# Two more modulation units from TensorE to VectorE beside the first mixer's heads, fed from the weights' buffers

## The chip, the cores and the metric

The kernel runs on one core of a Trainium2 chip. The metric is the device time of one execution in microseconds (us), taken as the median of several runs. The names used below are those of the profile: PE is TensorE, DVE is VectorE, ACT is ScalarE, POOL is GpSimd, and SP is the engine whose queue issues all the large DMAs.

## The reference

One inference step of a two-layer backbone. Both groups of 128 tokens (a prompt and a latent sample) pass through the same weights; the model width is 2048. Cut to what matters here:

```
for l in range(DEPTH):
    mod = jax.nn.silu(cond) @ w_ada[l] + b_ada[l]
    sh1, sc1, gt1, sh2, sc2, gt2 = jnp.split(mod[:, None, :], 6, axis=-1)
    h = rmsnorm(x, g_norm_mix[l]) * (1 + sc1) + sh1
    m, new = mixer_ab(h, ...) if l % 2 == 0 else mixer_c(h, ...)
    x = x + gt1 * m
    h = rmsnorm(x, g_norm_ffn[l]) * (1 + sc2) + sh2
    x = x + gt2 * conv_ffn(h, ...)
```

`mod` is a product of two condition vectors (one for each group) with a matrix of 2048 x 12288 per layer. It has only two rows of output, so its cost is that of bringing 100 MB of `w_ada` per layer through the core. It depends on nothing but the condition, so the kernel spreads it over the stages ahead of its use.

`mixer_ab` makes, from one input projection, queries and keys for eight heads of latent attention (which need two further small products, `w_q_up` and `w_kv_up`) and eight heads of grouped-query attention. An output projection `w_out` of 2048 x 2048 follows.

## The kernel before, in words

**Products.** Every weight tile of 128 x 2048 numbers (1024 KB) is loaded by SP into a buffer called `raw`, of which there are three, and then split in two halves of 1024 columns: ACT writes the rounded high part `wh` (L241), DVE the rest `wl` (L242). There are four buffers each for `wh` and `wl`. `gemm` (L393, L394, L397) then issues three matmuls for each block of 128 x 128. A product of the output projection, which will be called a chunk here, is 16 blocks and so 48 matmuls of 256 columns.

**Modulation units.** A unit is one of the six vectors of a layer, `j`, and a quarter of its 2048 outputs, `q`; it is four tiles of `w_ada`, 1024 KB each. There are three ways to do one.
- On PE (`row_step`, `sum_rows`, L526): a tile is loaded into one of two buffers `araw`; four matmuls with the condition as a narrow stationary matrix sum it into a PSUM tile, four column groups at a time; after four tiles ACT copies the result out, and four transposes (L477) turn it.
- On DVE by the row queue (units whose place in `ROWS` is in `SUMMED`): the tile is loaded in another layout, into the same `araw`, and DVE multiplies it with the condition, which lies in `condb` for each partition, and sums along the row (`feature_sum`, L503). A tile takes two such instructions, one for each condition vector.
- On DVE by the list `FEATS`, in the same way, from buffers of their own.

The rows of `ROWS` have numbers: 8 to 11 are the gate of the first mixer, 12 to 15 the scale of the first FFN, 16 and 17 half of its shift. Of these only unit 10 is in `SUMMED` before the change. The units are pushed on by `pump`, which stands after each product and advances the row queue by a rate (`RATE`, 0.85 in the heads, 0.7 in the output projection of this mixer; four steps to a tile at one step for 0.25).

**The heads** are the loop `for h in range(0, 8, 2)` of `mixer_ab`, from about 195 us of the profile on. Each of its four rounds has three products with `w_q_up`, two with `w_kv_up` and one by token for the values, and starts the attention of four heads. Their outputs go to `o`, a tile of 16 rows by the name `hx`; DVE's feature sums need a place for products that nobody reads, and took `o[:, 4:8]` for it until round h = 4.

**The output projection** follows: 16 chunks with `gemm(W.chunk(), oh, ol, first=8)`, each followed by `residual` (two DVE instructions, L667), by the row units that are left, and by two units of `FEATS` on DVE at 1.3 feature sums to a chunk. The last three chunks (`QUIET`) have none of these, and their splits are made in pieces of 512 columns. Then the sum of squares goes to PE (L221, L222), and the modulation of the FFN's input begins.

A scheduler orders the instructions of each engine ahead of time; where the code says `keep_in_program_order`, as for feature sums, the instruction keeps its place among others that say so. At run time each engine and the SP queue work strictly in that order.

Of the kernel before, what the change touches and what calls it, by code (L numbers as in the profile page):

```python
# [11 lines left out]
F32R = mybir.dt.float32r  # L12
# [6 lines left out]
P = 128  # L19
# [61 lines left out]
FEATS += [(1, 5, 1), (1, 5, 2), (1, 5, 3)]  # L81
RLIMIT = {"ab": 18, "ffn0": 19, "c": 30, "ffn1": 31}
FLIMIT = {"ab": 2, "ffn0": 14, "c": 14, "ffn1": 17}
SUMMED = [10, 20, 21, 22, 24, 25, 26, 29]
INV = {2048: 0, 768: 1, 512: 2, 128: 3, 256: 4}


# [1 line left out]
def step_kernel(ctx: ExitStack, tc: tile.TileContext, A: dict):  # L89
# [22 lines left out]
    def T_(pl, shape, tag, dt=F32, bufs=None):  # L112
        kw = {} if bufs is None else {"bufs": bufs}
        return pl.tile(shape, dt, tag=tag, name=nm(tag), **kw)
# [29 lines left out]
    act.activation(condw[:, :, 0:2], C("cond").rearrange("p (k r) -> p k r", r=2), AF.Silu)  # L144

    condb = T_(keep, [P, 2, D], "condb")

    def load_cw(l):
        ada["cw"] = T_(keep, [P, 4, 2 * NFF], "convw")
# [372 lines left out]
    def sum_rows(t, raw, ps=None):  # L522
        if t == 0:
            ada["ps"] = ps or T_(ppool["ada"], [P, 512], "ada", bufs=1)
        for g in range(4):
            i = pe.matmul(ada["ps"][32 * g:32 * g + 32, :], condw[:, 4 * t + g, :], raw[:, g],  # L526
                          start=(t == 0), stop=(t == 3), skip_group_check=True)
            if pinned[0]:
                tc.keep_in_program_order(i)

    def row_step(until=len(ROWS)):
        if later:
            later.pop(0)()
        if ada["i"] >= until:
            return
        l, j, q = ROWS[ada["i"]]
        t, g = divmod(ada["t"], 4)
        on_dve = ada["i"] in SUMMED
        if g == 0:
            ada["raw"] = T_(wpool, [P, 4, 512], "araw", bufs=2)  # L540
            sp.dma_start(out=ada["raw"], in_=A["w_ada"][l, j, q, t])
        raw = ada["raw"]
        if on_dve:
            if g % 2:
                feature_sum((l, j, q), t, g // 2, raw, ada["junk"]())
        elif pinned[0]:
            if g == 1 and t:
                sum_rows(t - 1, ada["last"])
            if g == 3:
                ada["last"] = raw  # L550
                if t == 3:
                    last = ada["last"]
                    later.append(lambda: None)
                    later.append(lambda: sum_rows(3, last))
        elif g == 3:
            sum_rows(t, raw)
        ada["t"] += 1
        if ada["t"] == 16:
            later.extend([lambda: biased(l, j, q)] if on_dve else ada_finish(l, j, q))
            ada["i"] += 1  # L560
            ada["t"] = 0

    def pump(rows, feats=0.0, until=None):

        until = until or RLIMIT[stage[0]]
        step()
        ada["due"] += rows
        while ada["due"] >= 0.25:
            if ada["i"] >= until and not later:
                ada["due"] = 0.0  # L570
                break
            dve_or_none = ada["i"] >= until or ada["i"] in SUMMED
            ada["due"] -= 0.25 if dve_or_none else 0.25 * ada["pew"]
            row_step(until)
        feat["due"] += feats
        while feat["due"] >= 1.0 and feat["i"] < FLIMIT[stage[0]]:
            feat["due"] -= 1.0
            feature_step()
# [46 lines left out]
    def modulated(st, l, which, W, fixed):  # L625
# [12 lines left out]
            return raw  # L638

        raws = [load_tile(0), load_tile(1)]  # L640
        hx = T_(keep, [P, KD, ROW], "hx", F32R)
        r = stat_rstd(st, D, att_bank)
        sum_rows(0, raws[0], bank())
        rb = spread(diagonal(r, (0, 1)), bank=att_bank)
# [91 lines left out]
    def mixer_ab(hx, W, units, st):  # L736
        l = 0
        with tc.tile_pool(name="ab", bufs=1) as ab:
# [275 lines left out]

            with tc.tile_pool(name="abh", bufs=1, reuse_waits="tile") as hp:
                ada["pew"] = PEW["heads"]
                ada["junk"] = lambda: o[:, 4:8]

                o = T_(keep, [P, KD, ROW], "hx", F32R)
                load_cw(0)  # L1020
                WQ = Weights(A["w_q_up"], 6, 2)
                WK = Weights(A["w_kv_up"], 4, 4)
# [29 lines left out]
                for h in range(0, 8, 2):  # L1052
                    for i in range(2):
                        ps = gemm(WQ.chunk(), qh, qlo)
                        qn[i] = T_(hp, [P, NT], "qn", bufs=3)
                        act.copy(qn[i], ps)
                        if h == 0:
                            for half in (slice(0, D // 2), slice(D // 2, D)):
                                act.activation(condb[:, i, half], condb[:, i, half], AF.Silu)
                        pump(RATE["heads"])  # L1060
# [3 lines left out]
                    qr = T_(hp, [P, NT], "qr", bufs=2)  # L1064
                    act.copy(qr[:, 0:T], ev[:, 0:T])
                    rope(qr[:, None, T:], ev[:, None, T:], 1, 32, "rcm", "rsm")
                    pump(RATE["heads"])
                    kn = []
                    for i in range(2):
                        if h + i < 7:  # L1070
                            start(gqa_query(h + i + 1))
                        start(gqa(h + i))
                        ps = gemm(WK.chunk(), kh, klo, 3 * T)
                        kn.append(T_(hp, [P, 3 * T], "kn", bufs=2))
                        act.copy(kn[i], ps)
                        pump(RATE["heads"])
                    if h == 0:
                        query_scale()
# [6 lines left out]
                        by_token(wide, xs, [out], True, True)  # L1085
                    act.copy(vs[:, :2 * NT], two)
                    act.copy(vs[:, 2 * NT:], one[:, :NT])
                    pump(RATE["heads"])
                    if h == 4:
                        ada["junk"] = None  # L1090
                    start(mla(h, qn[0], qr, kn[0], vm))
                    pump(RATE["heads"])
                    start(mla(h + 1, qn[1], qr, kn[1], vm))
                flush()
# [200 lines left out]
    with banks("pab") as ppool["ada"]:  # L1295
# [3 lines left out]
        for u in units[:2]:  # L1299
            u.load(1, tc.keep_in_program_order)  # L1300
            u.load(0, tc.keep_in_program_order)
            W.fetch(tc.keep_in_program_order)
        hx = T_(keep, [P, KD, ROW], "hx", F32R)
        st = stat_init()
        mixer_ab(hx, W, units, st)
        W = Weights(A["w_up"][0], KD, 1)
# [169 lines left out]
```

## Time and profile before

| what | value |
|---|---|
| runs | 2314.3, 2315.39, 2316.38 us; median 2315.39 |
| profiled execution, its own time | 2317.66 us |
| span in its profile | 2315.9 us |
| mean granted clock of PE | 0.993 |
| DVE busy | 1826.2 us (79%) |
| ACT busy | 1177.5 us (51%) |
| DMA | 610.82 MB, mean 264 GB/s |

The page of the profile says how busy each engine is over the span; the windows say the same for chosen stretches, with the granted clock, the mean busy share of the 16 DMA engines and the rate. A timeline lists instructions by start, with duration; where equal ones follow each other they are one row with a count, and the duration is then that of the whole row. Matmuls overlap, so what one costs is the distance from its start to the start of the next kind, not its duration. In these records a matmul of `L526` or of the attention stands twice: a tile's four matmuls are eight records.

### The profile page before, as it was taken

What the parts mean: (1) busy time and instruction counts of PE and PEld (TensorE: products, weight loads), DVE (VectorE), ACT (ScalarE), POOL (GpSimd) and SP (SyncE); (2) the same over time, 40 slices, a digit from 0 to 9 for tenths busy, and PEclk for the clock granted to TensorE, in tenths of its full rate; (3) what the DMA queues carried; (4) which work ended last, traced back from release to release, by engine and by line L of the source; (5) the groups of instructions that cost most, each with busy time, mean ns of one, the idle gap of its engine ahead of it and who ended that gap; (6) DMA issues with size and microseconds to landing.
All of it is one profiled execution on the core that took longest, in us unless ns stands there. A gap on an engine that the chain in (4) does not pass through costs nothing. (4 is left out here: it accounts for less than half of the span.)

```text
span 2315.9 us, 47404 instructions
## 1 busy us (share of the span) xinstructions
PE 2274.8 (98%) x19812; PEld 2183.7 (94%) x19812; DVE 1826.2 (79%) x2651; ACT 1177.5 (51%) x1869; POOL 145.9 (6%) x132
## 2 busy tenths in 40 slices
PE   8999999999999999999999999999999999999998
PEld 6888878799999999999989999898999999999998
DVE  5667749789989999999879989797899755666654
ACT  4347654555543455554465555446555434555553
POOL 0011101200000000002210000022000000000011
PEclk9999999999999999999999999999999999999999
DMA  9997889667768877777667788885667555555553
GB/s 391 386 370 274 300 310 394 239 250 258 258 253 308 291 259 271 256 260 274 267 244 280 285 316 293 297 307 220 251 247 266 199 186 198 199 186 198 196 188 127
DMA packets 92566, 610.82 MB, mean 264 GB/s; under 512 B 9984, under 2 KB 17856, under 8 KB 20544
## 3 DMA queue, kind: packets, MB, share of 16 engines
q1 hardware_dynamic: 92352, 607.80, 70.8%
q8 instruction: 155, 2.54, 0.4%
q14 instruction: 59, 0.48, 0.1%
HBM read 603.01 MB, written 4.75 MB: 262 GB/s over the span
## 5 line engine op out<-in xcount | busy, mean ns | idle before, releaser
L241 ACT CAST wh<-raw 128x1024 fp32r<-128x1024 f32 (+1 forms) x790 | 792.5, 1010 | 919.8 <-PE acc L394 700.2
L242 DVE TENSOR_TENSOR wl<-raw,wh 128x1024 fp32r<-128x1024 f32 (+1 forms) x790 | 923.7, 1185 | 300.7 <-ACT wh L241 292.5
L393 PE MATMUL acc<-hx,wh 128*128 128x256 f32 x3440 | 952.7, 277 | 1.4 <-ACT wh L241 0.8
L397 PE MATMUL acc<-hx,wl 128*128 128x256 f32 x3440 | 951.4, 277 | 0.2 <-DVE wl L242 0.2
L394 PE MATMUL acc<-hx,wh 128*128 128x256 f32 x3440 | 951.5, 277 | 0.0
L393 PEld LDWEIGHTS acc<-hx,wh 128*128 128x128 f32 x3440 | 646.1, 188 | 8.6 <-issue 5.9
L397 PEld LDWEIGHTS acc<-hx,wl 128*128 128x128 f32 x3440 | 645.5, 188 | 5.5 <-issue 3.4
L394 PEld LDWEIGHTS acc<-hx,wh 128*128 128x128 f32 x3440 | 646.2, 188 | 1.0 <-issue 0.8
L503 DVE CUSTOM_DVE_ANT_0 junk<-araw,condb 128x2048 f32<-128x2048 f32 (+1 forms) x192 | 442.7, 2306 | 0.1
L394 PE MATMUL acc<-g,wh 128*128 128x256 f32 x1408 | 388.3, 276 | 0.0
L397 PE MATMUL acc<-g,wl 128*128 128x256 f32 x1408 | 388.0, 276 | 0.0
L393 PE MATMUL acc<-g,wh 128*128 128x256 f32 x1408 | 387.8, 276 | 0.0
L394 PEld LDWEIGHTS acc<-g,wh 128*128 128x128 f32 x1408 | 264.3, 188 | 0.0
L397 PEld LDWEIGHTS acc<-g,wl 128*128 128x128 f32 x1408 | 264.2, 188 | 0.0
L393 PEld LDWEIGHTS acc<-g,wh 128*128 128x128 f32 x1408 | 264.1, 188 | 0.0
L190 POOL TENSOR_TENSOR sqacc<-sqacc,sq 128x256 f32<-128x256 f32 x61 | 81.8, 1341 | 1573.2 <-issue 1213.4
L914 PE MATMUL acc<-hx,wh 128*128 128x256 f32 x608 | 112.3, 285 | 1.0 <-ACT hx L884 0.6
L914 PEld LDWEIGHTS acc<-hx,wh 128*128 128x128 f32 x608 | 93.0, 189 | 9.4 <-issue 4.9
L1247 ACT ACTIVATE cv<-acc,convw 128x256 f32<-128x256 f32 x176 | 98.2, 558 | 2.5 <-PE acc L381 2.5
L667 DVE SCALAR_TENSOR_TENSOR x<-acc,mod,x 128x128 f32<-128x128 f32 x192 | 57.9, 342 | 40.9 <-PE acc L397 39.9
L1253 DVE SCALAR_TENSOR_TENSOR cv<-acc,convw,cv 128x254 f32<-128x254 f32 x176 | 84.3, 479 | 3.7
L1250 DVE SCALAR_TENSOR_TENSOR cv<-acc,convw,cv 128x254 f32<-128x254 f32 x176 | 83.5, 474 | 2.5 <-ACT cv L1247 2.5
(276 smaller groups left out, 2489.8 us busy)
## 6 DMA issues: line engine op xcount, KB each, us to landing
raw<-w_up SPq DMA_DIRECT2D x176, 1024.0 KB, 4.8
araw<-w_ada SPq DMA_DIRECT2D x160, 1024.0 KB, 5.3
raw<-w_down SPq DMA_DIRECT2D x88, 1024.0 KB, 4.8
raw<-w_in_c SPq DMA_DIRECT2D x48, 1024.0 KB, 5.6
raw<-w_in_ab SPq DMA_DIRECT2D x20, 1024.0 KB, 12.2
araw<-w_first SPq DMA_DIRECT2D x16, 1024.0 KB, 8.2
condb<-w_first SPq DMA_DIRECT2D x16, 1024.0 KB, 9.3
raw<-w_out_ab SPq DMA_DIRECT2D x16, 1024.0 KB, 7.8
```

The costliest lines, as they stand in the source:

```text
L190: pool.tensor_tensor(out=st["acc"], in0=st["acc"], in1=sq, op=ALU.add)
L241: pin(act.copy(out_hi, src))
L242: pin(dve.tensor_tensor(out=out_lo, in0=src, in1=out_hi.bitcast(F32), op=ALU.subtract))
L393: fixed(pe.matmul(ps[:, :n], wh, xh(k), start=(i == 0), stop=False))
L394: fixed(pe.matmul(ps[:, :n], wh, xl(k), start=False, stop=False))
L397: fixed(pe.matmul(ps[:, :n], wl, xh(k), start=False, stop=(i == last)))
L503: tc.keep_in_program_order(dve.tensor_tensor_reduce(out=junk, in0=raw, in1=condb[:, c].rearrange("p (g n) -> p g n", g=4), scale=1.0, scal ...
L667: dve.scalar_tensor_tensor(out=x[:, c, s], in0=ps[:, s], scalar=mod[:, l, 3 * which + 2, c, g:g + 1], in1=x[:, c, s], op0=ALU.mult, op1=AL ...
L914: pin(pe.matmul(ps, w, hx[:, k, lo:lo + NT], start=first and k == ks[0] and n == 0, stop=last and k == ks[-1] and n == 2, skip_group_check ...
L1247: pin(act.activation(y, ps, AF.Identity, scale=cw[:, 1, m:m + 1], bias=cw[:, 3, m:m + 1]))
L1250: pin(dve.scalar_tensor_tensor(out=y3[:, :, 1:], in0=p3[:, :, :T - 1], scalar=cw[:, 0, m:m + 1], in1=y3[:, :, 1:], op0=ALU.mult, op1=ALU.add))
L1253: pin(dve.scalar_tensor_tensor(out=y3[:, :, :T - 1], in0=p3[:, :, 1:], scalar=cw[:, 2, m:m + 1], in1=y3[:, :, :T - 1], op0=ALU.mult, op1=A ...
```

## The change

Units 10, 12 and 13 are named `APART`, and all three are now DVE's (only unit 10 was). They leave the row queue, which skips them, and have a queue of their own: `apart_step` does one feature sum, and stands at seven places in each round of the heads (four in the first round), so that 24 sums are spread over the heads. Their tiles are loaded by `apart_load` into a `raw` buffer, one of the three that the weights use, instead of `araw`. The first of these loads is issued before the heads' first weights. The place for products that nobody reads is now `hxb`, a part of `o` that the heads need last: `hx` is made as three tiles, `hxa` (rows 0 to 5), `hxb` (6 and 7) and `hxc` (8 to 15), that lie where the one tile lay.

```
-SUMMED = [10, 20, 21, 22, 24, 25, 26, 29]
+APART = [10, 12, 13]
+SUMMED = APART + [20, 21, 22, 24, 25, 26, 29]
...
+    class Rows:
+        STARTS = (0, 6, 8, KD)
+        def part(self, i):
+            if i not in self.tiles:
+                n = self.STARTS[i + 1] - self.STARTS[i]
+                self.tiles[i] = T_(keep, [P, n, ROW], "hx" + "abc"[i], F32R)
+            return self.tiles[i]
...
+    def skip():
+        while ada["i"] in APART and ada["t"] == 0:
+            ada["i"] += 1
+
+    def apart_load():
+        l, j, q = ROWS[APART[apart["n"] // 8]]
+        apart["raw"] = T_(wpool, [P, 4, 512], "raw")
+        sp.dma_start(out=apart["raw"], in_=A["w_ada"][l, j, q, apart["n"] % 8 // 2])
+
+    def apart_step():
+        if apart["n"] == 8 * len(APART):
+            return
+        unit = ROWS[APART[apart["n"] // 8]]
+        t, c = divmod(apart["n"] % 8, 2)
+        feature_sum(unit, t, c, apart["raw"], T_(keep, [P, 4, 512], "hxb", BF16))
+        apart["n"] += 1
+        if c and apart["n"] < 8 * len(APART):
+            apart_load()
+        if apart["n"] % 8 == 0:
+            biased(*unit)
...
-                ada["junk"] = lambda: o[:, 4:8]
-                o = T_(keep, [P, KD, ROW], "hx", F32R)
+                o = Rows()
+                o.part(0)
+                o.part(2)
+                apart_load()
                 load_cw(0)
                 WQ = Weights(A["w_q_up"], 6, 2)
...
                         act.copy(qn[i], ps)
+                        if h:
+                            apart_step()
...
                     rope(qr[:, None, T:], ev[:, None, T:], 1, 32, "rcm", "rsm")
+                    if h:
+                        apart_step()
                     pump(RATE["heads"])
...
                         act.copy(kn[i], ps)
+                        apart_step()
                         pump(RATE["heads"])
...
                     act.copy(vs[:, 2 * NT:], one[:, :NT])
+                    apart_step()
                     pump(RATE["heads"])
                     start(mla(h, qn[0], qr, kn[0], vm))
+                    apart_step()
                     pump(RATE["heads"])
```

Three places show how this moves instructions. In the rows that follow, the first word is the line of the code, and the arrow points from what is read to what is written.

The SP queue, from the last tile of the input projection on, before the change:

```order
L327 DMA raw_2160<-w_in_ab 128x1536
L287 DMA raw_2437<-w_q_up 128x1536
L541 DMA araw_2309<-w_ada 128x2048
L287 DMA raw_2512<-w_q_up 128x1536
L541 DMA araw_2388<-w_ada 128x2048
L287 DMA raw_2577<-w_kv_up 128x2048
L800 DMA o_ckv<-proj_122 512x1x128
L287 DMA raw_2822<-w_q_up 128x1536
L848 DMA o_gqa_v<-vg_116 128x256
L287 DMA raw_2927<-w_kv_up 128x2048
L838 DMA o_gqa_k<-kg_115 256x1x128
```

The same place in the changed kernel (L566 is the load of a tile that is summed apart, L176 loads the FFN's convolution weights):

```order
L353 DMA raw_2162<-w_in_ab 128x1536
L566 DMA raw_2435<-w_ada 128x2048
L176 DMA convw_2437<-wconv 128x352
L591 DMA araw_2311<-w_ada 128x2048
L313 DMA raw_2442<-w_q_up 128x1536
L591 DMA araw_2390<-w_ada 128x2048
L313 DMA raw_2517<-w_q_up 128x1536
L851 DMA o_ckv<-proj_124 512x1x128
L899 DMA o_gqa_v<-vg_118 128x256
L889 DMA o_gqa_k<-kg_117 256x1x128
L313 DMA raw_2582<-w_kv_up 128x2048
```

A tile of the separate queue is now the first of them, and the first `w_kv_up` tile has moved from ahead of the three stores to behind them.

DVE in the output projection, from the fifth residual to the sixth and on to the next feature sum, before (L242 is a split, L503 a feature sum in two rows, L479, L487 and L492 finish units):

```order
L667 SCALAR_TENSOR_TENSOR x_75<-acc_4182,mod_81,x_75 128x128 x2
L242 TENSOR_TENSOR wl_4334<-raw_4327,wh_4333 128x1024
L503 ISA junk_4170,mod_81<-araw_4168,condb_89 128x2048
L503 ISA mod_81 128x1
L479 TENSOR_REDUCE mod_81<-ada_4242 128x8
L242 TENSOR_TENSOR wl_4403<-raw_4400,wh_4402 128x1024
L667 SCALAR_TENSOR_TENSOR x_75<-acc_4262,mod_81,x_75 128x128 x2
L487 TENSOR_TENSOR mod_81<-mod_81,cst_74 128x8
L242 TENSOR_TENSOR wl_4407<-raw_4400,wh_4406 128x1024
L492 SCALAR_TENSOR_TENSOR scl_82<-mod_81,cst_74 128x8
L503 ISA junk_4250,mod_81<-araw_4168,condb_89 128x2048
```

And in the changed kernel:

```order
L718 SCALAR_TENSOR_TENSOR x_75<-acc_4256,mod_81,x_75 128x128 x2
L268 TENSOR_TENSOR wl_4387<-raw_4380,wh_4386 128x1024
L529 ISA junk_4310,mod_81<-araw_4242,condb_89 128x2048
L529 ISA mod_81 128x1
L268 TENSOR_TENSOR wl_4454<-raw_4451,wh_4453 128x1024
L718 SCALAR_TENSOR_TENSOR x_75<-acc_4322,mod_81,x_75 128x128 x2
L268 TENSOR_TENSOR wl_4458<-raw_4451,wh_4457 128x1024
L529 ISA junk_4378,mod_81<-araw_4376,condb_89 128x2048
```

The large instructions are the same; only the three small ones that finish a PE unit have gone.

DVE at the end of the output projection, from the fourteenth residual on, before:

```order
L667 SCALAR_TENSOR_TENSOR x_75<-acc_4857,mod_81,x_75 128x128 x2
L503 ISA junk_4840,mod_81<-araw_4766,condb_89 128x2048
L503 ISA mod_81 128x1
L242 TENSOR_TENSOR wl_4982<-raw_4979,wh_4981 128x512 x2
L242 TENSOR_TENSOR wl_4988<-raw_4979,wh_4987 128x512 x2
```

And in the changed kernel, from the last feature sum but one:

```order
L529 ISA junk_4787,mod_81<-araw_4785,condb_89 128x2048
L529 ISA mod_81 128x1
L268 TENSOR_TENSOR wl_4995<-raw_4992,wh_4994 128x512 x2
L718 SCALAR_TENSOR_TENSOR x_75<-acc_4870,mod_81,x_75 128x128 x2
L268 TENSOR_TENSOR wl_5001<-raw_4992,wh_5000 128x512 x2
L529 ISA junk_4853,mod_81<-araw_4785,condb_89 128x2048
```

The splits of the last chunk (128x512) stood behind the last feature sum and now stand ahead of it.

On PE the 32 tiles of units 9 and 11 to 17 were spread from the heads to the end of the output projection, and 24 are left. Counted in the order of instructions from the heads' first product on: up to the first matmul of the output projection there stood 14 tile sums and 4 turns of a unit, and now 24 and 6; up to the end of its first chunk 21 and 6, and now 24 and 7; behind that 11 and 3, and now none.

More of the change, by code (lines that the diff above doesn't have):

```diff
@@ L146, in step_kernel, with __init__, made, __getitem__ @@
     condb = T_(keep, [P, 2, D], "condb")
+    class Rows:
+        STARTS = (0, 6, 8, KD)
+        def __init__(self):
+            self.tiles = {}
+        def part(self, i):
[3 more added lines that the diff above has]
+            return self.tiles[i]
+        def made(self):
+            for i in range(3):
+                self.part(i)
+            return self
+        def __getitem__(self, at):
+            p, k, *rest = at
+            i = max(i for i in range(3) if self.STARTS[i] <= k)
+            return self.part(i)[(p, k - self.STARTS[i], *rest)]
     def load_cw(l):
@@ L529, in sum_rows @@
                 tc.keep_in_program_order(i)
+    def skip():
+        while ada["i"] in APART and ada["t"] == 0:
+            ada["i"] += 1
+    apart = {"n": 0, "raw": None}
+    def apart_load():
[13 more added lines that the diff above has]
+            biased(*unit)
     def row_step(until=len(ROWS)):
+        skip()
         if later:
@@ L568, in pump @@
         while ada["due"] >= 0.25:
+            skip()
             if ada["i"] >= until and not later:
@@ L640, in modulated @@
         raws = [load_tile(0), load_tile(1)]
-        hx = T_(keep, [P, KD, ROW], "hx", F32R)
+        hx = Rows().made()
         r = stat_rstd(st, D, att_bank)
@@ L1087, in mixer_ab @@
                     act.copy(vs[:, 2 * NT:], one[:, :NT])
+                    apart_step()
                     pump(RATE["heads"])
-                    if h == 4:
-                        ada["junk"] = None
                     start(mla(h, qn[0], qr, kn[0], vm))
+                    apart_step()
                     pump(RATE["heads"])
@@ L1302, in step_kernel @@
             W.fetch(tc.keep_in_program_order)
-        hx = T_(keep, [P, KD, ROW], "hx", F32R)
+        hx = Rows().made()
         st = stat_init()
```

## The prediction

> **What bounds the kernel now.** I read the page first, for the engine that limits the whole.
>
> ```profile
> span 2315.9 us, 47404 instructions
> PE 2274.8 (98%) x19812; PEld 2183.7 (94%) x19812; DVE 1826.2 (79%) x2651; ACT 1177.5 (51%) x1869; POOL 145.9 (6%) x132
> ```
>
> By the page PE is the bound and DVE has 21% to spare, so work moved from PE to DVE looks like gain. That is an average. The change touches only 195 to 430 us, so the windows there come next: the heads, the tail of attention with the first chunk, the output projection, the boundary behind it, and two stretches inside.
>
> ```profile
> core 0: us, PE busy (x) PEld busy (x) DVE busy (x) ACT busy (x) POOL busy (x), PEclk, DMA share, GB/s
> 195.00:299.00 104.00, 102.29 (x783) 87.60 (x782) 73.44 (x177) 66.00 (x161) 9.81 (x9) 1.00 0.75 278
> 299.00:335.00 36.00, 34.38 (x275) 26.96 (x275) 11.38 (x32) 17.92 (x44) 0.00 (x0) 1.00 0.85 335
> 335.00:412.00 77.00, 76.01 (x644) 66.93 (x643) 75.96 (x93) 32.49 (x47) 14.88 (x13) 1.00 0.96 375
> ...
> 421.00:430.00 9.00, 6.49 (x40) 2.70 (x33) 5.23 (x15) 5.77 (x10) 1.64 (x1) 0.80 0.69 242
> 360.00:400.00 40.00, 40.00 (x342) 35.17 (x342) 39.69 (x50) 16.00 (x22) 7.65 (x7) 1.00 1.01 407
> 217.00:247.00 30.00, 29.61 (x240) 28.76 (x238) 28.87 (x48) 19.99 (x44) 4.35 (x4) 1.00 0.69 250
> ```
>
> Three different limits stand here. In the heads PE is busy 102.29 of 104 us and DVE 73.44: room on DVE. In the output projection (335 to 412) both are full, PE 76.01 and DVE 75.96 of 77, and so is the DMA at 0.96. From 421 PE idles: a chain of small steps sets the time. So an instruction taken from PE pays in the heads, and in the projection only as far as DVE can follow.
>
> **What goes from PE.** The prices are distances between starts.
>
> ```profile
> 211.99 1.06 PE L526 MATMUL ada<-araw,condw 128*32 128x512 f32 x8
> 212.99 0.38 PE L361 MATMUL acc<-wl,kv_in 128*128 128x256 f32 x1
> ...
> 197.93 0.60 PE L477 MATMUL ada<-cst,am 128*128 128x128 f32 x4
> 198.28 0.37 PE L393 MATMUL acc<-ql,wh 128*128 128x256 f32 x1
> ```
>
> A tile costs 1.00 us (211.99 to 212.99), a turn 0.35 to 0.45 with the slower matmul behind it; I take 0.45. A unit is 4.45 and the two units 8.9 us of PE. The order in the section on the change says where: PE's remaining tiles move forward. Up to the end of the first chunk it now has 24 tiles and 7 turns for 21 and 6, and behind that none for 11 and 3.
>
> **Term 1, to the first residual.** Three tiles and a turn more are 3.45, and ten matmuls of a later chunk that now stand ahead, at 0.117 each (40 us with 342 in the window 360 to 400), 1.1: **+4.6**. (The heads alone, to the first matmul of the projection, grow by ten tiles and two turns, about 11; the tail behind them shrinks by nearly as much.)
>
> **Term 2, the projection.** PE loses 11 tiles and 3 turns here, 12.4 us. What DVE loses is read from its groups from 334 to 416 us.
>
> ```profile
> L503 DVE CUSTOM_DVE_ANT_0 junk<-araw,condb 128x2048 bf16<-128x2048 f32 x16 | 39.8, 2485 | 0.1
> L242 DVE TENSOR_TENSOR wl<-raw,wh 128x1024 fp32r<-128x1024 f32 x20 | 25.4, 1276 | 2.4 <-ACT wh L241 2.4
> L667 DVE SCALAR_TENSOR_TENSOR x<-acc,mod,x 128x128 f32<-128x128 f32 x30 | 9.0, 340 | 0.7 <-PE acc L397 0.7
> L242 DVE TENSOR_TENSOR wl<-raw,wh 128x512 fp32r<-128x512 f32 x12 | 8.6, 771 | 0.0
> ```
>
> Sums, splits and residuals are 82.8 us, and all stay: the two units that DVE gains are done in the heads, and the 16 sums of the list `FEATS` remain here. Only the instructions that finish PE's units go, about 1 us, and of DVE's idle time perhaps the 1 us that is left in the window 335 to 412. So DVE sets the end, and the last residuals show how.
>
> ```profile
> 335.19 0.60 DVE L667 SCALAR_TENSOR_TENSOR x<-acc,mod,x 128x128 f32<-128x128 f32 x2
> ...
> 409.64 0.61 DVE L667 SCALAR_TENSOR_TENSOR x<-acc,mod,x 128x128 f32<-128x128 f32 x2 [0.70 <-PE acc L397]
> 410.17 2.28 DVE L503 CUSTOM_DVE_ANT_0 junk<-araw,condb 128x2048 bf16<-128x2048 f32 x1
> ...
> 412.37 3.02 DVE L242 TENSOR_TENSOR wl<-raw,wh 128x512 fp32r<-128x512 f32 x4
> 415.39 0.59 DVE L667 SCALAR_TENSOR_TENSOR x<-acc,mod,x 128x128 f32<-128x128 f32 x2
> ```
>
> The first residual starts at 335.19, the fourteenth at 409.64: 74.45 us. In the changed kernel two of the last chunk's four splits (3.02 for four) stand ahead of the fourteenth: 74.45 - 2 (the us of small instructions and the us of idle time) + 1.5 = 73.95. Behind it come the residual (0.6) and the other two splits (1.5), and then PE has half a chunk, 24 matmuls or 2.8 us, and some 0.4 to start on it: 79.2 from the first residual to PE's end.
>
> ```profile
> 420.20 0.28 PE L397 MATMUL acc<-hx,wl 128*128 128x256 f32 x1
> 420.41 1.07 PE L526 MATMUL ada<-araw,condw 128*32 128x512 f32 x8
> 421.72 1.06 PE L526 MATMUL ada<-araw,condw 128*32 128x512 f32 x8
> 422.71 0.38 PE L222 MATMUL att<-cst,sq 128*128 128x1 f32 x2
> ```
>
> Before, the projection's last matmul starts at 420.20, 85.0 behind the first residual. The gain is **-5.8** of PE's 12.4. If nothing of DVE's idle time went it would be -4.8; if DVE kept no one waiting, PE's 12.4 less the 2.4 of the next term, -10.
>
> **Term 3, the boundary.** The last two tiles stand between that matmul and L222, the sum of squares that the chain needs. Both go, with a turn behind, 2.4 us of PE; but L222 has the last residual to wait for as well, so I take **-0.9**, with 0 and -2.3 (420.41 to 422.71) as ends.
>
> **Term 4, new waits in the heads.** First the stores. The first `w_kv_up` tile is now behind three of them in the SP queue, and the third waits for keys that the heads' beginning makes.
>
> ```profile
> 186.55 0.38 SPq L287 DMA_DIRECT2D raw<-w_kv_up  x1
> ...
> 199.39 0.57 SPq L838 DMA_DIRECT2D o_gqa_k<-kg  x1
> ```
>
> The list of DMA issues has the time from issue to landing (the last column), the timeline PE's first use, and the groups of ACT and DVE in the heads the splits and sums:
>
> ```profile
> raw<-w_kv_up SPq DMA_DIRECT2D x4, 1024.0 KB, 5.9
> ```
> ```profile
> 203.98 0.42 PE L393 MATMUL acc<-kv_in,wh 128*128 128x384 f32 x1
> ```
> ```profile
> L241 ACT CAST wh<-raw 128x1024 fp32r<-128x1024 f32 x15 | 15.7, 1046 | 8.4 <-PE acc L394 8.4
> ```
> ```profile
> L242 DVE TENSOR_TENSOR wl<-raw,wh 128x1024 fp32r<-128x1024 f32 x16 | 19.5, 1222 | 4.6 <-ACT wh L241 4.6
> L503 DVE CUSTOM_DVE_ANT_0 hx<-araw,condb 128x2048 fp32r<-128x2048 f32 x8 | 18.2, 2280 | 1.4 <-DMA araw<-w_ada 1.4
> ```
>
> Issued at 200.0 for 186.55, landed 5.9 later, its first half split at ACT in 1.0 and at DVE in 1.2, it is whole at 208.1. PE uses it from 203.98 on, in the changed order about a us later, since some attention matmuls now stand ahead: it would wait for the high part until 206.9, about 2, and nearly nothing again for `wl`. I take 1.5. Behind PE's first `w_kv_up` matmul stands everything in program order.
>
> Second, DVE gets sixteen more sums of 2.28 us, 36.5 beside its 73.44, in heads that grow to about 115: 110. It still fits, but DVE's work comes in stretches. Where it already had eight sums (217 to 247, DVE 28.87 of 30 us) PE lost 0.39 us; at that density throughout the heads, 1.5. Together **+3**. The lower end is -3.2, if no new wait comes and the two old ones go:
>
> ```profile
> PE ada L526 <- DMA araw<-w_ada: 1.9, 2, 1.5
> PE att L730 <- ACT pT L707: 1.3, 1, 1.3
> ```
>
> The upper end is DVE bound: of its 30.6 us of idle time, mostly waits for ACT and PE, half stays, 110 + 15 for 115: **+10**. DMA tells about the same. From the last load of the input projection (178.2) to the second chunk's, SP has 47.25 tiles of 1024 KB to bring (0.75 of that load, 4.5 of `w_q_up`, 4 of `w_kv_up`, 12 apart, 24 for PE, 2 of the projection), 49.5 million bytes. At the 407 GB/s of 360 to 400 us that is 122 us, until 300, ten before the heads' end at 310; at the 375 of 335 to 412 it is 132, until 310. One of three `raw` buffers is in most moments held by a tile that waits for its sums, so the loads have less lead than now.
>
> [...]
>
> A sum in the heads takes 2.28 us and in the projection 2.49 in the mean. The long ones there fall together with POOL:
>
> ```profile
> 350.64 2.82 DVE L503 CUSTOM_DVE_ANT_0 junk<-araw,condb 128x2048 bf16<-128x2048 f32 x1
> ```
> ```profile
> 350.24 1.07 POOL L190 TENSOR_TENSOR sqacc<-sqacc,sq 128x256 f32<-128x256 f32 x1 [5.61 <-ACT sq L189]
> ```
>
> So the sum moved to the heads, where POOL does little, is priced at 2.28. [...] With 2.82 throughout the heads would have 8.6 us more of DVE, and come near the upper end above.
>
> **The sum.** 4.6 - 5.8 - 0.9 + 3 = +0.9 on the profiled execution's 2317.66: 2318.6. That execution is 2.3 above the median of the runs, so in their terms **2316.3**. A measurement can tell about 0.2%, 4.6 us, from no change; this is no change.
>
> **Rivals.**
> - *PE stays the only bound.* The heads bear the sums without a wait, and PE's order alone counts: -8.9 of work, of which the 2.4 at the boundary pay 0.9 only: -7.4, 2308. For it speaks PE's 98%, and that the buffers `wl` give PE some lead over DVE. Against it DVE's 75.96 of 77 with work that stays.
> - *DVE and the loads become the bound of the heads.* Term 4 takes its upper end: 4.6 - 5.8 - 0.9 + 10 = +7.9, 2323. It decides from the point where a tile apart cannot be summed within the round in which it holds its `raw` buffer: weights then land late, ACT and DVE split late, PE waits. For it: 110 of 115 us on DVE, one buffer of three. Against it: the 30 us in which DVE did eight sums and PE lost next to nothing.
> - *The end of the projection does not follow.* Should the last splits wait for their load (the DMA is at 0.96 to 1.01) rather than for DVE, term 2 is halved: +3.8, 2319. It is within the forecast's range.
>
> **Chances and range.** The forecast, 2311 to 2321 with its own bounds, 0.46; PE alone the bound, 0.26; heads bound by DVE and loads, 0.28. The range goes from 2307 (PE alone, and part of the old waits gone) to 2324. Faster by over 0.2%: 0.27; within: 0.46; slower: 0.27.
>
> **What would show it.** Of the changed kernel: the projection's first matmul at 310 to 313 us (299 before); the first residual at about 343; DVE over 98% busy from there on, with PE now idle a few us for `wl`, and PE's last chunk done at about 422; a wait of PE at 205 to 208 for the first `w_kv_up` tile. I am wrong if PE has no gaps in the projection (then DVE had room, and the result is faster), or if PE in the heads waits over 5 us for splits or loads (slower).

## The result, and the profile after

| | before | changed |
|---|---|---|
| median | 2315.89 us (4 runs) | 2334.19 us (4 runs, 2331.33 to 2334.95) |
| ratio of the runs | | 1.0077, 95% interval 1.006 to 1.0094 |
| profiled execution, own time | 2317.66 | 2331.33 (the fastest of its four) |
| PE's first product of the heads | 195.1 | 196.2 |
| first residual of the projection | 335.2 | 353.4 |
| PE's last matmul of the projection | 420.2 | 434.3 |
| first matmul of the FFN behind it | 429.4 | 444.4 |
| mean granted clock from 195 us to the first residual | 1.00 | 0.98 |

The change makes the kernel slower by 18 us; no change was forecast, and the time lies outside the range. The starts in the table are read from the timelines. They put the loss in one place: the first residual is 18.2 us late, the projection takes 80.9 in place of 85.0, the boundary 10.1 in place of 9.2, and the rest of the kernel 1885.2 in place of 1886.5: 18.2 - 4.1 + 0.9 - 1.3 = 13.7, the difference of the two profiled executions. The other 4.6 of the 18.3 between the medians are spread between executions, and no profile shows them.

The page of the changed kernel, first lines:

```profile
span 2329.6 us, 47279 instructions
PE 2272.3 (98%) x19740; PEld 2183.4 (94%) x19740; DVE 1860.4 (80%) x2681; ACT 1177.2 (51%) x1867; POOL 138.1 (6%) x132
```

PE is as good as ever at 98%, and only 2.5 us less busy though 8.9 us of work are gone; the page hides the loss as it hid the limits before. Its windows, from 195 us to the first residual and from there to the last (columns: stretch, length, busy time of PE, PEld, DVE, ACT and POOL, granted clock, DMA share, GB/s):

```profile
195.00:353.40 158.40, 147.71 (x1100) 118.99 (x1099) 120.74 (x251) 87.23 (x210) 7.67 (x9) 0.98 0.87 336
353.40:436.90 83.50, 75.14 (x633) 73.84 (x631) 83.47 (x100) 36.39 (x50) 18.20 (x14) 0.98 0.66 240
```

In the projection DVE is busy 83.47 of 83.50 us and PE waits for it: that part went as forecast. Ahead of it PE is idle 10.7 us of 158.4, where before it was 3.2. What PE waited for there (waits of PE, 195 to 353 us: total, times, longest):

```profile
PE acc L423 <- DVE wl L268: 3.8, 4, 2.2
PE acc L419 <- ACT wh L267: 2.0, 2, 1.2
PE ada L552 <- DVE mod L505: 1.9, 1, 1.9
PE att L756 <- ACT p L774: 1.6, 1, 1.6
PE att L766 <- DVE hxa L268: 1.2, 1, 1.2
```

All five name DVE or ACT, and 5.8 of the us are splits of weights that came late. Before, PE waited for no split in the heads (its two rows there are in the prediction). Over 5 us of such waits is what the prediction named as its sign of being wrong on the slow side. One of them, followed back in the timeline of the changed kernel:

```profile
228.92 2.27 DVE L529 CUSTOM_DVE_ANT_0 hxb<-raw,condb 128x2048 bf16<-128x2048 f32 x1
...
231.22 0.33 SPq L313 DMA_DIRECT2D raw<-w_kv_up  x1
...
238.81 1.99 ACT L267 CAST wh<-raw 128x1024 fp32r<-128x1024 f32 x2
...
241.00 2.28 DVE L529 CUSTOM_DVE_ANT_0 hxb<-raw,condb 128x2048 bf16<-128x2048 f32 x1
...
243.94 1.23 DVE L268 TENSOR_TENSOR wl<-raw,wh 128x1024 fp32r<-128x1024 f32 x1
...
245.22 0.45 PE L423 MATMUL acc<-kv_in,wl 128*128 128x384 f32 x1 [2.24 <-DVE wl L268]
```

The load of `w_kv_up` is issued at 231.22, just as a sum apart ends on DVE at 231.2, the second one of a tile that was loaded at 201.84. The weight lands 7.6 us behind its issue, and ACT splits it from 238.81; DVE then is in another sum until 243.3 and writes `wl` from 243.94; PE has stood since 243.0 and goes on at 245.22. So a tile apart delays a weight twice: it sits in a buffer that the weight's load needs, and its sum stands ahead of the weight's split. The first of these is no single case: the weights' loads at 221.72, 248.75, 288.67, 320.47 and 332.14 are also issued 0.03 or 0.04 us behind the second sum of a tile apart, and each of the six tiles had been in its buffer for 19 to 42 us, counted from the issue of its load. ACT's own waits in the heads (195 to 335 us) say how often a weight had not landed:

```profile
ACT wh L267 <- DMA raw<-w_kv_up: 7.3, 3, 3.5
...
ACT wh L267 <- DMA raw<-w_q_up: 1.0, 1, 1.0
```

Before, ACT has no such row at all. Then there is something that the prediction did not have. Four windows around the wait on `L505`, each as long as a step of the clock's record:

```profile
308.44:311.85 3.41, 2.60 (x20) 1.96 (x16) 3.37 (x8) 1.09 (x3) 0.00 (x0) 1.00 1.00 406
311.85:315.25 3.40, 1.59 (x11) 0.69 (x12) 3.37 (x8) 1.62 (x2) 0.00 (x0) 1.00 0.97 383
315.25:318.66 3.41, 3.41 (x14) 1.28 (x13) 3.36 (x7) 1.46 (x5) 0.00 (x0) 0.50 1.01 413
318.66:322.07 3.41, 3.41 (x21) 3.41 (x21) 2.32 (x5) 1.18 (x3) 0.00 (x0) 1.00 0.89 320
```

PE waits, is busy 1.59 of 3.40 us, and then has half its clock (0.50) for 3.41 us: 1.7 us of work lost, reckoned as half of that. This stands at 274.3, 315.3 and 359.6, and in the kernel before not once between 195 and 426. Some waits were paid twice.

### The profile page after: what moved, and what is told of

It reads as the page before. It is cut to its first block, busy times and chain, and to the rows that moved or that the text cites. A ratio compares the mean times of both kernels' runs of the same rounds, so it can differ in the third digit from the quotient of the medians.

```text
span 2329.6 us, 47279 instructions
## 1 busy us (share of the span) xinstructions
PE 2272.3 (98%) x19740; PEld 2183.4 (94%) x19740; DVE 1860.4 (80%) x2681; ACT 1177.2 (51%) x1867; POOL 138.1 (6%) x132
## 5 line engine op out<-in xcount | busy, mean ns | idle before, releaser
L423 PE MATMUL acc<-hxc,wl 128*128 128x256 f32 x1720 | 477.2, 277 | 5.0 <-DVE wl L268 5.0
L419 PE MATMUL acc<-hxc,wh 128*128 128x256 f32 x1720 | 476.3, 277 | 2.2 <-DVE x L718 2.0
L420 PE MATMUL acc<-hxc,wh 128*128 128x256 f32 x1720 | 476.2, 277 | 0.0
L419 PE MATMUL acc<-hxa,wh 128*128 128x256 f32 x1290 | 358.6, 278 | 3.8 <-ACT cv L1304 3.3
L423 PE MATMUL acc<-hxa,wl 128*128 128x256 f32 x1290 | 357.1, 277 | 0.0
L420 PE MATMUL acc<-hxa,wh 128*128 128x256 f32 x1290 | 356.8, 277 | 0.0
L423 PEld LDWEIGHTS acc<-hxc,wl 128*128 128x128 f32 x1720 | 323.6, 188 | 8.6 <-DVE wl L268 6.0
L419 PEld LDWEIGHTS acc<-hxc,wh 128*128 128x128 f32 x1720 | 323.5, 188 | 3.4 <-ACT sqacc L207 2.2
L420 PEld LDWEIGHTS acc<-hxc,wh 128*128 128x128 f32 x1720 | 323.7, 188 | 0.0
L419 PEld LDWEIGHTS acc<-hxa,wh 128*128 128x128 f32 x1290 | 242.8, 188 | 5.1 <-ACT cv L1304 3.4
L420 PEld LDWEIGHTS acc<-hxa,wh 128*128 128x128 f32 x1290 | 242.4, 188 | 0.2
L423 PEld LDWEIGHTS acc<-hxa,wl 128*128 128x128 f32 x1290 | 242.4, 188 | 0.0
```

What stands on the lines that cost most here:

```text
L419: fixed(pe.matmul(ps[:, :n], wh, xh(k), start=(i == 0), stop=False))
L420: fixed(pe.matmul(ps[:, :n], wh, xl(k), start=False, stop=False))
L423: fixed(pe.matmul(ps[:, :n], wl, xh(k), start=False, stop=(i == last)))
```

## The experiments

Two theories at first. **A**: the sums' time on DVE makes PE wait. **B**: the tiles apart make weights land late; B1 by the `raw` buffer that they hold and the SP queue that stands still for it, B2 by their bytes. C was that PE's tiles moved into the heads are the loss. In the table, PE's idle time is the sum of its idle stretches over 0.1 us from the heads' first product to the first residual, and half clock the time at 0.50 up to there, both from the timelines and the clock's record; the third column is ACT's wait for weights to land, from 195 to 335 us (where the first residual comes later, nothing is added up to there). The heads start between 194.0 and 196.6 us in these runs, without a pattern by what they load, and the first residual moves with that.

| run | median us, ratio with interval | first residual | ACT waits for weights | PE idle | half clock |
|---|---|---|---|---|---|
| before | | 335.2 | 0 | 3.2 | 0 |
| changed | 2334.2, 1.0077 (1.006 to 1.0094) | 353.4 | 8.3 | 10.7 | 6.8 |
| x1_no_loads | 2318.1, 1.0012 (1.0002 to 1.0021) | 341.5 | 0 | 3.5 | 6.8 |
| x2_thin_sums | 2325.2, 1.0042 (1.0028 to 1.0056) | 343.8 | 2.4 | 6.7 | 3.4 |
| x3_rate50 | 2330.3, 1.0064 (1.0049 to 1.0079) | 350.5 | 10.4 | 13.3 | 20.5 |
| x4_araw | 2357.4, 1.018 (1.0165 to 1.0196) | 377.1 | 0 | 33.6 | 47.8 |
| x5_small_loads | 2329.8, 1.0064 (1.0047 to 1.008) | 350.6 | 14.5 | 10.5 | 3.4 |
| x6_early_free | 2318.0, 1.0006 (0.9996 to 1.0015) | 338.5 | 1.3 | 4.0 | 6.8 |
| x7_pairs | 2340.3, 1.0101 (1.0086 to 1.0116) | 362.9 | 12.5 | 14.6 | 17.1 |
| x9_nearly_free | 2316.2, 0.9998 (0.9989 to 1.0007) | 336.9 | 0 | 0 | 0 |
| y0_row12 | 2322.1, 1.0025 (1.0016 to 1.0034) | 342.8 | 0 | 10.3 | 10.2 |
| z1_apart10 | 2324.2, 1.003 (1.0019 to 1.0042) | 343.0 | 3.0 | 3.4 | 3.4 |
| y1_row11 | 2327.0, 1.0044 (1.003 to 1.0058) | 343.6 | 0 | 10.8 | 13.6 |
| z2_apart10_12 | 2327.3, 1.005 (1.0036 to 1.0063) | 346.7 | 4.7 | 7.3 | 3.4 |
| y8_row12_thin | 2312.8, 0.9983 (0.9974 to 0.9992) | 333.3 | 0 | 5.4 | 0 |

### Loads or sums

```diff
-        apart["raw"] = T_(wpool, [P, 4, 512], "raw")
-        sp.dma_start(out=apart["raw"], in_=A["w_ada"][l, j, q, apart["n"] % 8 // 2])
+        apart["raw"] = condb[:, 1].rearrange("p (g n) -> p g n", g=4)
```

> The 24 sums that stand apart read data that lies in the core (the second condition row) in place of a loaded tile: no loads for them and no raw buffer held; DVE's instructions and PE's order are those of the changed kernel. Left out: the true values of three modulation units. Theory A (DVE's time: the sums make splits, turns and reductions late, and PE waits): first residual stays at 350 to 354 us, PE still waits 8 us or more ahead of it, time 2329 to 2335. Theory B (loads and the raw buffer: weights land late): first residual at 342 to 345, PE waits under 5 us, time about 2322.

12 us of the 18 at the first residual go, 2.2 of them because the heads of this execution start earlier. That is close to the 342 to 345 of B, and far from A's 350. DVE is as busy as in the changed kernel (the window from 195 us to the first residual):

```profile
195.00:341.50 146.50, 143.00 (x1085) 117.88 (x1084) 117.98 (x246) 82.21 (x202) 14.63 (x9) 0.98 0.73 274
```

117.98 us of DVE in 146.50, where the changed kernel has 120.74 in 158.40: all 24 sums are there, and PE waits no longer. So the sums' time on DVE alone does not cost what the change costs. Thin sums, with the loads kept:

```diff
-        feature_sum(unit, t, c, apart["raw"], T_(keep, [P, 4, 512], "hxb", BF16))
+        feature_sum(unit, t, c, apart["raw"], T_(keep, [P, 4, 512], "hxb", BF16), 64)
```

> The 24 sums that stand apart take 64 of each 512 columns, so each lasts some 0.35 us in place of 2.28; the loads, the raw buffer and PE's order stay. Left out: seven eighths of three modulation units. Theory A: DVE has 46 us less in the heads, first residual at 341 to 344, no dip of the granted clock there, time about 2321. Theory B: first residual at 349 to 353, PE still waits for splits whose tiles landed late, time 2328 to 2334.

9.6 us go: the first residual is where A had it, though weights still land late (2.4) and the time, 2325, lies between the two. A shorter sum also frees its buffer sooner (in the changed kernel the weights' loads were issued 0.03 or 0.04 us behind a sum's end), so this run alone does not tell A from B1.

### Bytes or buffer

```diff
-        sp.dma_start(out=apart["raw"], in_=A["w_ada"][l, j, q, apart["n"] % 8 // 2])
+        sp.dma_start(out=apart["raw"][:, 0:1], in_=A["w_ada"][l, j, q, apart["n"] % 8 // 2][:, 0:1])
...
+        junk = T_(keep, [P, 4, 512], "hxb", BF16)
+        feature_sum(unit, t, c, condb[:, 1].rearrange("p (g n) -> p g n", g=4), junk, 1, 3)
+        feature_sum(unit, t, c, apart["raw"], junk, 0, 1)
```

> The tiles apart are loaded by a quarter (256 KB in place of 1024); each sum is made of two instructions, three quarters on data that lies in the core and one quarter on what was loaded, so the raw buffer is held and freed by DVE as in the changed kernel, and DVE's time is a little longer. Left out: the true values of three modulation units. Theory B1 (the raw buffer that is held, and the SP queue that stands still for it, make weights late): first residual at 348 to 354 us, time 2327 to 2335. Theory B2 (the bytes: 12 tiles more beside PE's in the heads slow every transfer): first residual at 341 to 344, time about 2319.

```diff
         sp.dma_start(out=apart["raw"], in_=A["w_ada"][l, j, q, apart["n"] % 8 // 2])
+        pool.tensor_tensor(out=T_(apart["pool"], [P, 4], "freed"), in0=apart["raw"][:, :, 0], in1=apart["raw"][:, :, 1], op=ALU.subtract)
...
-        feature_sum(unit, t, c, apart["raw"], T_(keep, [P, 4, 512], "hxb", BF16))
+        feature_sum(unit, t, c, condb[:, 1].rearrange("p (g n) -> p g n", g=4), T_(keep, [P, 4, 512], "hxb", BF16))
```

> The tiles apart are loaded whole into a raw buffer, as in the changed kernel, but a tiny GpSimd instruction reads them and frees the buffer as soon as they land; DVE's 24 sums read data that lies in the core. Bytes and DVE's time as in the changed kernel, the hold ends earlier. Left out: the true values of three modulation units. In order, PE has 21 tiles and 6 turns up to the end of the first chunk here (24 and 7 in the changed kernel). B1: first residual at 336 to 341 us, time 2313 to 2320. B2: 346 to 351, time 2324 to 2332.

These two are opposite, and they settle it for B1. A quarter of the bytes with the same hold changes little (350.6, 2329.8), and of the 2.8 us at the first residual 2.2 are an earlier start of the heads. All the bytes with the buffer freed at landing takes 15 of the 18 us away (338.5, 2318.0), of which 3.4 are the three tiles and a turn that this kernel's order has fewer and 1.4 an earlier start. ACT's waits for weights, with small loads:

```profile
ACT wh L267 <- DMA raw<-w_q_up: 6.3, 3, 2.9
ACT wh L267 <- DMA raw<-w_kv_up: 5.4, 4, 3.6
ACT wh L267 <- DMA raw<-w_out_ab: 2.8, 1, 2.8
```

and with the early release:

```profile
ACT wh L267 <- DMA raw<-w_kv_up: 1.3, 1, 1.3
```

Weights land late by 14.5 us in the sum where quarter tiles hold their buffers until DVE has summed them, and by 1.3 where whole tiles give them up at landing.

### More of the hold, less of it, another buffer

```diff
-APART = [10, 12, 13]
+APART = [10]
```

> Only unit 10 apart: the queue and its hold of a raw buffer, without a new unit on DVE; units 12 and 13 stay on PE. In order PE has 25 tiles and 7 turns up to the end of the first chunk (21 and 6 before), 4.5 us more, and 7 tiles behind. Theory B1: eight sums hold a raw buffer in the first half of the heads, waits of PE on splits of 3 to 6 us there, first residual at 342 to 347 us, time 2320 to 2326. If the hold costs nothing: 339 to 341, and 2313 to 2317, since the projection has three tiles less.

```diff
-APART = [10, 12, 13]
+APART = [10, 12]
```

> Units 10 and 12 apart, 13 on PE: the same two units on DVE as in the run with unit 12 in the row queue, but with their tiles in raw buffers. Nothing is left out. In order, 25 tiles and 7 turns up to the end of the first chunk. Theory B1: eight sums more that hold a raw buffer, a few us of waits on splits above the run with unit 10 alone: first residual at 346 to 352 us, time 2326 to 2331. If the hold matters little: as the run with unit 10 alone, 342 to 344 and 2320 to 2324, since the projection loses three more tiles.

Both times and first residuals lie in the ranges of B1: with one, two and three units apart ACT waits 3.0, 4.7 and 8.3 us for weights, and the medians are 2324.2, 2327.3 and 2334.2. With unit 10 alone no new unit is on DVE at all: the queue with its buffer, and the 4.5 us of PE tiles that it lets move ahead, cost 7.6 us. But the hold is the smaller part of that. PE waits for splits once, for 2.2 us and not for 3 to 6, and is idle no longer than before (3.4 for 3.2); of the 7.8 us at the first residual 4.5 are the tiles, 1.2 a later start of the heads, and 1.7 the half clock.

```diff
+        apart["turn"] = not apart.get("turn", True)
+        if apart["turn"]:
+            return
+        apart_one()
+        apart_one()
```

> Both sums of a tile apart are made at one place, at every second of the places, so the buffer is held for a shorter time and its tile has longer to land. Nothing is left out. B1: first residual at 343 to 349 us, time 2320 to 2328. B2: as the changed kernel, 351 to 354, 2329 to 2335.

```diff
-        apart["raw"] = T_(wpool, [P, 4, 512], "raw")
+        apart["raw"] = T_(wpool, [P, 4, 512], "araw", bufs=2)
```

> The tiles that are summed apart are loaded into the two araw buffers, which PE's tiles use too, so weights have three raw buffers for themselves again. Theory A: no change, first residual at 350 to 356, 2329 to 2337. Theory B, by the raw buffer: PE's waits for splits go, first residual at 344 to 348, 2323 to 2328, though PE's own tiles may now wait for araw.

Both were misses. Pairs made it worse (weights late by 12.5 us): the two sums of a tile now mostly follow each other on DVE within 0.8 us (nine of the twelve pairs), so that a split behind them waits for some 4.6 us, and in the SP queue two loads apart came to stand directly behind each other; which of these costs more was not tried. With `araw` no weight is late any more, as B1 has it, but PE's tiles then wait for that buffer instead (waits of PE up to 380 us):

```profile
PE ada L552 <- DMA araw<-w_ada: 32.2, 8, 7.5
```

### The rate, and what the work on PE is worth

```diff
-RATE = {"in3": 0.25, "heads": 0.85, ...
+RATE = {"in3": 0.25, "heads": 0.5, ...
```

> The changed kernel with the heads' rate of the row queue at 0.5 in place of 0.85: in order, 15 tiles and 4 turns on PE up to the end of the projection's first chunk in place of 24 and 7 (21 and 6 before), and 9 tiles left in the projection (11 before, none in the changed kernel). Theory C (what was lost is PE's tiles that moved into the heads, where they wait and share the loads, while the projection is bound by DVE and gains nothing): first residual at 329 to 335, projection about 85 us, time 2309 to 2316. Theory A or B alone, waits as in the changed kernel: first residual at 342 to 345, time 2322 to 2327.

C falls: with nine tiles and three turns fewer ahead of the first residual, 10.4 us of PE, it comes only 2.9 earlier. The 342 to 345 of the other two, with the waits of the changed kernel, was missed as well: PE's idle time rises to 13.3 and half clock to 20.5 us. Here work taken from an engine that waits for late weights became idle time, and idle time became half clock.

```diff
-        sp.dma_start(out=apart["raw"], in_=A["w_ada"][l, j, q, apart["n"] % 8 // 2])
+        apart["raw"] = condb[:, 1].rearrange("p (g n) -> p g n", g=4)
...
-        feature_sum(unit, t, c, apart["raw"], T_(keep, [P, 4, 512], "hxb", BF16))
+        feature_sum(unit, t, c, apart["raw"], T_(keep, [P, 4, 512], "hxb", BF16), 0, 64)
```

> The sums apart read data in the core, 64 of each 512 columns, and nothing is loaded: two units taken from PE at almost no cost elsewhere. Left out: three modulation units. It shows what the removed PE work is worth. If DVE bounds the projection (the prediction's term 2): first residual at 338 to 341 us, from there to the last matmul 79 to 82, time 2312 to 2316. If PE bounds it: 73 to 75 from the first residual, time 2304 to 2309.

No wait is left in the heads, and the time is that of before, 2316.2. The first residual comes 1 us earlier than its range, and the last matmul 82.6 us behind it, 0.6 above the range for DVE as the bound and far from PE's 73 to 75. The projection's window, from the first residual on:

```profile
336.90:420.50 83.60, 77.22 (x630) 76.07 (x629) 83.54 (x99) 36.25 (x50) 23.44 (x14) 0.94 0.66 240
```

DVE is busy 83.54 of 83.60 us, and PE has half its clock for 10.2 us there (0.94 in the mean) without a price, since DVE has no gap. So even for nothing, two units taken from PE bring nothing as long as PE's tiles move ahead into the heads and the projection is left to DVE.

### One unit by the row queue

```diff
-APART = [10, 12, 13]
-SUMMED = APART + [20, 21, 22, 24, 25, 26, 29]
+APART = []
+SUMMED = [10, 12, 20, 21, 22, 24, 25, 26, 29]
...
-                apart_load()
+                ada["junk"] = lambda: T_(keep, [P, 4, 512], "hxb", BF16)
```

> The other way to give DVE a unit: no queue apart; unit 12 joins unit 10 in the row queue (loads into araw at the place where PE's tile was loaded, the raw buffers left to the weights), with the products that nobody reads in the rows hxb. Nothing is left out. In order, PE has 17 tiles and 5 turns up to the end of the first chunk (21 and 6 before), and as many behind it as before; DVE has eight sums more in the second half of the heads, where it idles. Theory B1 (what cost time was the held raw buffer): PE's 4.45 us go where PE is the bound, first residual at 330 to 332 us, time 2310 to 2313. Theory A (DVE's sums themselves make PE wait): first residual at 334 to 340, time 2315 to 2322.

No weight is late, as B1 has it, and still the first residual comes 7.6 us later than before, beyond the range of A too. The waits of PE in the heads name one place:

```profile
PE att L756 <- ACT p L774: 6.3, 1, 6.3
```

DVE's timeline there:

```profile
281.23 2.29 DVE L529 CUSTOM_DVE_ANT_0 hxb<-araw,condb 128x2048 bf16<-128x2048 f32 x1
...
284.57 0.23 DVE L747 SCALAR_TENSOR_TENSOR nmx<-mx,rsb 128x2 f32<-128x2 f32 x2
...
287.37 2.29 DVE L529 CUSTOM_DVE_ANT_0 hxb<-araw,condb 128x2048 bf16<-128x2048 f32 x1
...
290.72 0.16 DVE L773 RECIPROCAL rec<-sums 128x2 f32<-128x2 f32 x1
```

The windows of the wait and of the stretch behind it:

```profile
285.30:288.70 3.40, 0.00 (x0) 0.00 (x0) 3.31 (x7) 2.61 (x9) 0.00 (x0) 1.00 0.48 135
288.70:298.90 10.20, 6.97 (x28) 4.62 (x28) 9.18 (x20) 3.65 (x10) 0.00 (x0) 0.50 0.59 202
```

One attention head goes to and fro between the engines: maximum (`nmx`) on DVE, exponent on ACT, reciprocal (`rec`) on DVE, scaling on ACT, transposes on PE. A sum and splits stand ahead of `nmx`, and again ahead of `rec`. PE idles 6.3 us, has no work at all in 285.3 to 288.7, and then half its clock for 10.2 us. The wait reaches into that stretch, where PE is busy 6.97 us: 6.3 and half of 6.97 are 9.8 us at this one place. (The next expectation reckons 11.4, with half of all 10.2, and so counts a part of the wait twice.) So A is true as well, of another kind than first thought: not DVE's sum of time, but a link that stands behind 2.3 us of other work.

```diff
-SUMMED = [10, 12, 20, 21, 22, 24, 25, 26, 29]
+SUMMED = [10, 11, 20, 21, 22, 24, 25, 26, 29]
```

> As the run with unit 12 in the row queue, but unit 11 in its place: the eight new sums follow those of unit 10 at once, about 20 us earlier, so other instructions of DVE stand behind them. Nothing is left out. In order, PE has 17 tiles and 5 turns up to the end of the first chunk, as there. In the run with unit 12, no load was late, but one attention head's chain (maximum, exponent, reciprocal, scaling) stood behind three sums on DVE: PE idled 6.3 us at one place and then had half the clock for 10.2 us, 11.4 together. If that is an accident of the place: first residual at 330 to 334 us here, time 2310 to 2314. If any sum among the heads' short instructions costs as much (theory A in its new form): first residual at 338 to 344, again a wait of PE on the attention's ACT or DVE steps of over 3 us, time 2317 to 2324.

It is no accident of the place: again one wait of 6.4 us for `p`, at 253.2, and again 10.2 us of half clock, which begins within it. The first residual, 343.6, is in the range of the second case; the time, 2327.0, is 3 above it.

```diff
     def feature_sum(unit, t, c, raw, junk):
+        n = 64 if unit[:2] == (0, 4) else 512
...
-            out=junk, in0=raw, in1=condb[:, c].rearrange("p (g n) -> p g n", g=4), ...
+            out=junk[:, :, :n], in0=raw[:, :, :n], in1=condb[:, c].rearrange("p (g n) -> p g n", g=4)[:, :, :n], ...
```

> The run with unit 12 in the row queue, with its eight sums on 64 of each 512 columns: some 0.35 us in place of 2.28 each. Loads, buffers and PE's tiles (17 and 5 turns up to the end of the first chunk) as there. Left out: seven eighths of unit 12. If DVE's time among the attention's short instructions was the whole loss there: no wait of PE over 2 us in the heads, no half clock there, first residual at 330 to 332 us, time 2310 to 2313. If the unit's removal moves something else (loads, the order on PE): first residual at 335 or more, 2315 or more.

The waits of PE in the heads, first row:

```profile
PE ada L553 <- DMA araw<-w_ada: 1.7, 3, 0.8
```

No wait over 1 us, no half clock, 2312.8 and a ratio of 0.9983 (0.9974 to 0.9992). The first residual is 1.3 us later than the range given, the time inside it. With loads, buffers and PE's order alike (only the `araw` buffers should come free sooner behind a shorter sum, which was not measured apart), the sums' 15 us on DVE (an estimate: eight at 2.28 less the 0.35 expected) are worth 9.5 us of the first residual, or 8.3 from the start of the heads on, which is 1.3 earlier here. This run is faster than before because it leaves most of one unit out; it shows what a unit taken from PE would bring if it cost the heads nothing on DVE, 4 us. No kernel here that does all the work beats the one before.

## Why the prediction was wrong, point by point

- **Term 1 (+4.6)** stood, if a little large. PE's order was read rightly, and the run in which the two units cost almost nothing has the first residual at 336.9: 1.7 later than before, of which 1.4 is a later start of the heads, while 3.2 us of idle time that before had are gone. That is 3.5 of work by difference.
- **Term 2 (-5.8)** had the right mechanism and was a little too large: -4.1. DVE has no idle time from the first residual on, but its busy time up to the last residual rose from 81.25 us (335.2 to 420.8 before) to 83.47, where the forecast had it fall by 1. Its sums took 2589 ns and its splits 1310 in the mean, against 2485 and 1276, which the forecast took. The 0.4 that its sum allows PE to start on a split is shown by no run; at 245.22 PE went on 0.05 us behind the split that it waited for. The sums and splits:

```profile
L529 DVE CUSTOM_DVE_ANT_0 junk<-araw,condb 128x2048 bf16<-128x2048 f32 x16 | 41.4, 2589 | 0.0
L268 DVE TENSOR_TENSOR wl<-raw,wh 128x1024 fp32r<-128x1024 f32 x22 | 28.6, 1310 | 0.0
```

  In the same stretch before, the sums were 39.8 us, the splits of 1024 columns 26.7 (21 of them) and those of 512 columns 8.6, now 7.7. The sums are longer where they meet POOL: nine of the sixteen took 2.82 us or a little more, six before, and each of these starts while a POOL instruction is running. Two during which one starts (at 367.82 and 386.66) took 2.28.
- **Term 3 (-0.9)** had the wrong sign: +0.9. The two tiles did go from in front of the sum of squares, but DVE, now the bound, does the last residual 2.6 us behind PE's last matmul (434.3 to 436.9; 0.6 before), and the chain waits for that.
- **Term 4 (+3, at most +10)** is the step that failed: 18.2 - 4.6 = 13.6. Its first part, the stores ahead of `w_kv_up`, did not come: PE starts there at 206.46 without a wait. The second part was priced by how dense DVE already was in 217 to 247 us, where PE lost 0.39 us. But there a sum's tile lay in `araw`, out of the weights' way; the density was the same kind of row, the buffer another. The rival "DVE and the loads become the bound" named the mechanism, a weight late because a tile apart holds its buffer, and the runs with small loads and with early release show it. It had too low a price: 7.5 us more of idle PE (10.7 for 3.2), 3.4 us lost to half clock (6.8 at 0.50), 1.1 that the heads start later, which may be no work of the change (194.0 to 196.6 in the other runs). 1.6 stay without a name, and 2.7 if term 1 is taken at the 3.5 that was measured.
- **The rival "PE stays the only bound"** fell in both parts: the heads did wait, and the projection followed DVE.
- The prediction's argument that DVE "still fits", 110 of 115 us, was right as a sum (117.98 of 146.50 with no late weight) and beside the point: what mattered was where in the order each sum stands.

That the half clock makes up 3.4 of the 13.6 is reckoned from the clock's record and PE's work at 0.50; no run took the clock away alone.

## What to carry to other kernels

A buffer borrowed from a prefetch ring (the few buffers into which weights are loaded ahead of their use) was paid by the ring here: with a quarter of the bytes and the same hold the first residual came at 350.6 us, with all the bytes and the buffer freed at landing at 338.5, against 353.4. So ask not how many bytes the newcomer loads, but which instruction releases its buffer, how late that one stands on its engine, and which loads queue behind it. Moving work to an engine with idle time asks for the place of each piece too: with unit 12 in the row queue two short links of a chain, 0.23 and 0.16 us, stood behind sums of 2.29, and PE idled 6.3 us for it. And before work is taken from the busiest engine, look which engine bounds each stage: where another is as full, as DVE with 83.54 of 83.60 us in the run that made the sums nearly free (2316.2 us), the work must come out of the other stages.

## What the hardware showed beside that

PE's granted clock fell to 0.50 after quite short waits, for 3.41 us or several times that (10.24 at 426.4 in the kernel before, 10.2 in the runs with unit 12 and with unit 11 in the row queue). From 150 us on every such stretch in the traces of the kernel before (three) and of the changed one (six) begins within 0.004 us of one grid of 3.413 us. In the changed kernel three of them stand behind idle stretches of 1.57, 1.89 and 2.0 with 1.08, in steps of the grid in which PE was about half busy (1.75, 1.59 and 1.69 of 3.40 to 3.42).

Yet the waits of 2.24 us at 243.0 and 388.4 in the same profile had no half clock behind them, so the length alone does not tell. The place on the grid is a part of it. With unit 10 alone PE has the same wait of 2.24 us, at 243.1: there it falls into one step (241.68 to 245.10, PE busy 1.41 of 3.42), and half clock follows; in the changed kernel it spreads over two (busy 2.82 and 1.76 of 3.41). Counted over the traces of the kernel before and of the changed one from 150 to 2250 us, of the 14 steps at full clock in which PE was busy for 2.19 us or less, seven were followed by half clock, and of the 1201 others none. Busy time is not all of it: the wait at 388.4 left PE busy 1.50 of 3.42 without half clock behind it, half clock at 1160.3 in the kernel before follows a step with 2.19 of 3.41 busy, and in the run with early release half clock at 253.0 follows one with 3.01 of 3.41 and no wait over 0.32. What else decides was not tried.

In the sums of the projection POOL and DVE stretched each other. In the changed kernel each of the nine sums that start while a POOL addition runs took 2.82 to 2.84 us, and each of the other seven 2.28 or 2.29 (376.70, POOL from 376.31 for 1.07). Where the sum starts first it took 2.28, and POOL's addition 2.14 and 2.13 in place of 1.07 (367.82, POOL from 368.56; 386.66, POOL from 387.40).
